# A two-layer trunk kernel: the blocked down-projection over 20 tiles of features in one pass, sums of activations made in the up-projection

## Chip, cores and metric

The kernel runs on one core of a Trainium2 chip. The metric is the device time of one execution in microseconds (us); lower is better.

## What is computed

The reference is a two-layer trunk over 1024 prompt tokens and 8 x 4 sample tokens, 1056 columns in all, with a model width of 1024. In each layer a mixer, a cross-attention and a convolutional feed-forward part follow one another. The change concerns the feed-forward part alone:

```python
def conv_ffn(h, w_up, conv_w, conv_b, w_down, prev):
    L = h.shape[1]
    up = h @ w_up                                  # 1024 -> 2 * 2816
    ext = jnp.concatenate([prev.astype(up.dtype), up], axis=1)
    c = conv_b + conv_w[0] * ext[:, 0:L]
    for j in range(1, CONV_W):                     # CONV_W = 3
        c = c + conv_w[j] * ext[:, j:j + L]
    a, b = jnp.split(c, 2, axis=-1)
    y = (jax.nn.silu(a) * b).astype(h.dtype)
    return y @ w_down, ext[:, L:]                  # 2816 -> 1024, added to x
```

## The kernel before

Every fp32 product is made of three matmuls (`mm3`): each operand is split into a rounded high part and the low rest, high by high, high by low and low by high (L594, L595, L596). ScalarE (ACT) makes a high part by a copy, VectorE (DVE) the low part by a subtraction.

**Blocks.** In most of the feed-forward part a 2 x 2 block scheme with seven products in place of eight is used. `PRODUCTS` names for each product p the part or sum of weights (a11, a12, s1 to s4, a22), the part or sum of activations (b11, b21, b22, t1 to t4) and the accumulator. Blocks of weights pair two tiles of 128 rows or columns; blocks of activations are half of the 1056 columns (528, two pieces c of 264). The order of the products in a block is p = 1, 2, 6, 5, 7, 3, 4, each for c = 0 and 1: 14 steps. `Blocks.steps` makes the sums of weights on GpSimd (POOL; L233, L234, L235, L239) and their parts (ACT L219, DVE L220); the names are `wru`/`wsu` for raw and summed weights and `whiu`, `wh1u`, `whsu`, `w4u` and so on for parts, with a `d` at the end in the down-projection.

**Up-projection.** 22 tiles of features (f = 0 to 21), each with its gate tile. Tiles 1 to 21 are blocks of 14 steps of 12 matmuls of 128x264 into `blu`. `ffn_take` empties a step's bank into `ext`: ACT copies (L964) after p = 1, 6 and 5, DVE adds (L968) after p = 2, 7 and 3 with a scaling on POOL behind (L969), and one DVE multiply (L966) after p = 4. There are three banks for these, so product 3 waits for the copy that empties product 5. `ffn_conv` queues the convolution of a finished tile in `self.slow`: a first tap on ACT (L1005), two more on DVE (L1008), silu on ACT (L1012) and the product on DVE (L1014, and L1018 for the 32 sample columns), which is stored to `fd` in DRAM. `tick` hands this queue out behind the next tile's steps, by a credit of time. So while PE works on tile f, the other engines convolve tile f - 1.

**Down-projection.** Five groups of four tiles of features (`GROUPS`), each group fetched from `fd`, its seven activation operands made (sums on POOL L723 and L724 and on DVE L726 and L727, parts L519 and L520), and multiplied into four pairs of output tiles: 5 x 4 blocks of 14 steps of 6 matmuls, 1680 a layer, into `bld`. `ffn_add` adds every step's bank to the residual rows `xff`, once or twice: on DVE (L984), or for p = 1 and 6 by an ACT copy into `dtd` (L981) and a POOL add (L982). The last two tiles of features (20 and 21) follow in `out_last` (`ogd_e`), which isn't changed.

Programs are written in the order of the calls; each engine runs its instructions in that order, and DMAs are issued from one queue (SP). Nothing is reordered on the chip.

## Time and profile before

| | |
|---|---|
| median of 3 runs | 3243.94 us (3241.47 to 3248.48) |
| profiled execution | 3238.84 us, of which its span is 3237.1 us |
| up-projection's steady part, layer 0 | within 1100 to 1360 us of the span |
| down-projection by blocks, layer 0 and 1 | from 1399.9 and 2958.4 us to 1633.2 and 3188.6 us |

The span is the time from the first to the last instruction in the trace; 1.7 us of the execution lie around it. PE is TensorE's matmul stream and PEld its weight loads; the trace's times are in us from the start of the span. A row of a timeline gives start, duration, engine, line, operation, written tile, read tiles, shapes, and in square brackets how long the engine stood idle ahead of it and who released it.

### The profile page before, as it was taken

To read this page: it belongs to the slowest core of one execution; us is meant where nothing else is said; L and a number is where in the kernel's file an instruction comes from. 1 tells how busy PE (TensorE), PEld (TensorE's weight loads), DVE (VectorE), ACT (ScalarE), POOL (GpSimd) and SP (SyncE) were. 2 spreads that over 40 slices of the span, in tenths; PEclk is the share of its full clock that TensorE was granted. 3 is DMA by queue.
4 is the path that set the end of the run, shared out by engine and by line. 5 is a ranking of instruction groups with operands and counts; after the bars stand their busy time and mean duration, and the time that the engine had idled before them with its cause. 6 is when DMAs were issued, how large, how long until landed. Compare 5 with 4: busy or idle time off the path is not lost. (4 is left out here: it accounts for less than half of the span.)

```text
span 3237.1 us, 65350 instructions
## 1 busy us (share of the span) xinstructions
PE 3101.1 (96%) x25741; PEld 2952.3 (91%) x25741; DVE 2446.9 (76%) x4662; ACT 1454.7 (45%) x3008; POOL 1468.3 (45%) x1722
## 2 busy tenths in 40 slices
PE   8999899999989999999999999899999999999998
PEld 6998888998889999988989999889989899999998
DVE  6649977834798888899974444675378988889998
ACT  7223255444464444444442333244445544444445
POOL 5011113300457777778731111240025677777874
PEclk9999999999999999999999999999999999999999
DMA  8513264344222222242231111225333222224322
GB/s 267 187 47 97 80 206 159 107 147 139 89 89 84 82 81 75 74 154 96 83 119 55 47 55 52 76 75 178 111 126 102 73 82 82 79 77 152 101 73 97
DMA packets 367072, 336.08 MB, mean 104 GB/s; under 512 B 30029, under 2 KB 317948, under 8 KB 366764
## 3 DMA queue, kind: packets, MB, share of 16 engines
q1 hardware_dynamic: 366764, 331.90, 32.1%
q8 instruction: 202, 3.31, 0.4%
q14 instruction: 106, 0.87, 0.1%
HBM read 250.60 MB, written 81.24 MB: 103 GB/s over the span
## 5 line engine op out<-in xcount | busy, mean ns | idle before, releaser
L969 POOL TENSOR_TENSOR ext<-ext,rstdff 128x264 f32<-128x264 f32 (+2 forms) x336 | 358.7, 1093 | 122.2 <-DVE ext L968 121.9
L1008 DVE SCALAR_TENSOR_TENSOR ct<-ext,cw,ct 128x528 f32<-128x528 f32 (+1 forms) x352 | 370.5, 1089 | 47.4 <-ACT ct L1005 45.6
L1005 ACT ACTIVATE ct<-ext,cw 128x544 f32<-128x544 f32 (+1 forms) x176 | 141.7, 833 | 212.1 <-POOL ext L969 96.2
L596 PE MATMUL blu<-hhff,wlou 128*128 128x264 f32 x672 | 191.8, 286 | 3.6 <-DVE wlou L220 3.6
L594 PE MATMUL blu<-hhff,whiu 128*128 128x264 f32 x672 | 191.5, 286 | 0.0
L982 POOL TENSOR_TENSOR xff<-xff,dtd 128x264 f32<-128x264 f32 x160 | 159.8, 1011 | 63.8 <-ACT dtd L981 63.0
L723 POOL TENSOR_TENSOR o<-o 128x528 f32<-128x528 f32 x4 | 5.4, 1342 | 360.1 <-DVE xo1bb L272 179.4
L984 DVE TENSOR_TENSOR xff<-xff,bld 128x264 f32<-128x264 f32 x400 | 154.3, 417 | 6.7 <-PE bld L596 5.2
L596 PEld LDWEIGHTS blu<-hhff,wlou 128*128 128x128 f32 x672 | 127.2, 189 | 4.0 <-DVE wlou L220 4.0
L964 ACT COPY ext<-blu 128x264 f32<-128x264 f32 (+2 forms) x336 | 98.3, 323 | 65.0 <-PE blu L596 62.9
L594 PEld LDWEIGHTS blu<-hhff,whiu 128*128 128x128 f32 x672 | 127.5, 190 | 0.0
L594 PE MATMUL pjxq<-hhxa,whxq 128*128 128x352 f32 x384 | 126.3, 329 | 0.0
L595 PE MATMUL pjxq<-hlxa,whxq 128*128 128x352 f32 x384 | 125.5, 327 | 0.0
L596 PE MATMUL pjxq<-hhxa,wlxq 128*128 128x352 f32 x384 | 124.8, 325 | 0.0
L968 DVE TENSOR_TENSOR ext<-ext,blu 128x264 f32<-128x264 f32 (+2 forms) x336 | 104.4, 350 | 0.0
L595 PE MATMUL blu<-hhff,whiu 128*128 128x264 f32 x336 | 96.6, 288 | 0.0
L596 PE MATMUL blu<-hhff,w4u 128*128 128x264 f32 x336 | 95.7, 285 | 0.0
L595 PE MATMUL blu<-hlff,w4u 128*128 128x264 f32 x336 | 95.7, 285 | 0.0
L594 PE MATMUL blu<-hhff,w4u 128*128 128x264 f32 x336 | 95.6, 285 | 0.1
L595 PE MATMUL blu<-hlff,whiu 128*128 128x264 f32 x336 | 95.6, 285 | 0.0
L219 ACT CAST w4u<-wru 128x512 fp32r<-128x512 f32 x42 | 26.1, 621 | 149.9 <-POOL wru L239 141.6
L1400 POOL TENSOR_TENSOR khg<-khg,tothg 128x512 f32<-128x512 f32 (+1 forms) x24 | 31.8, 1325 | 123.1 <-PE shg L1371 53.1
(2690 smaller groups left out, 13083.5 us busy)
## 6 DMA issues: line engine op xcount, KB each, us to landing
wru<-in_ffn_w_up SPq DMA_DIRECT2D x88, 512.0 KB
wrd<-in_ffn_w_down SPq DMA_DIRECT2D x80, 256.0 KB
wrkv<-in_xa_w_kv SPq DMA_DIRECT2D x32, 512.0 KB
kc<-in_cache_mem_k SPq DMA_DIRECT2D x64, 256.0 KB
vc<-in_cache_mem_v SPq DMA_DIRECT2D x64, 256.0 KB
fd<-ct SPq DMA_DIRECT2D x44, 264.0 KB
fd<-ct SPq DMA_DIRECT2D x44, 248.0 KB
xmx<-xd SPq DMA_DIRECT2D x16, 528.0 KB
```

Of the source, the lines that this page charges most:

```text
L219: nc.scalar.copy(out=hi, in_=src)
L594: nc.tensor.matmul(ps, wh, ah, start=first, stop=False, **kw)
L595: nc.tensor.matmul(ps, wh, al, start=False, stop=False, **kw)
L596: nc.tensor.matmul(ps, wl, ah, start=False, stop=last, **kw)
L964: nc.scalar.copy(out=d, in_=z)
L968: nc.vector.tensor_tensor(out=d, in0=d, in1=z, op=ALU.add)
L969: nc.gpsimd.tensor_tensor(out=d, in0=d, in1=r, op=ALU.mult)
L982: nc.gpsimd.tensor_tensor(out=x, in0=x, in1=b, op=ALU.add)
L984: nc.vector.tensor_tensor(out=x, in0=x, in1=ps, op=ALU.add)
L1005: nc.scalar.activation(out=ct[q], in_=exts[q][0][:, o:o + w], func=AF.Identity, scale=wv(0, q), bias=wv(3, q))
L1008: nc.vector.scalar_tensor_tensor(out=ct[q], in0=exts[q][0][:, o + j:o + j + w], scalar=wv(j, q), in1=ct[q], op0=ALU.mult, op1=ALU.add)
L1400: nc.gpsimd.tensor_tensor(out=kv, in0=kv, in1=tv[:, :, 1:2].to_broadcast([P, nb, m]), op=ALU.mult)
```

## The change

The down-projection by blocks is one pass over the 20 tiles: `DOWN` puts its seven products outermost; for each there are two halves of the output (`mp`, two pairs of output tiles) and three cuts of the ten pairs of features (`CUTS`: 4, 3 and 3). A product accumulates over all ten pairs in its own banks, and only then `take` adds it to the residual: 48 adds on DVE into `xff`, 16 into `ud` and 16 ACT copies into `ud`, and 8 POOL adds of 528 columns in a layer stand for the 200 DVE and 80 POOL adds of 264 columns and the 80 ACT copies of before. There are still 1680 matmuls a layer. The weights come in pieces of 384 or 512 KB, and since a piece serves one product, some blocks are loaded two or three times: 23.6 MB for 10.5 MB a layer. Sums of weights on POOL and the columns of their parts stay as many.

The sums of activations t1 to t4 are made in the up-projection, as 40 instructions of 128x528 a layer on POOL: one for an even tile (`first_sum`), three for an odd one (`other_sums`), put into `self.slow` ahead of the next tile's convolution. The seven operands are stored to DRAM (`bd`) as 7 x 10 half blocks of 270 KB, and fetched and split product by product (5 fetches of 540 KB and 10 splits of 528 columns for each), one product ahead. The 80 such sums of before in the down-projection (half on POOL, half on DVE, both layers) fall away.

```diff
...
-NSLOT = 40
+NSLOT = 43
...
-GROUPS = [2,2,2,2,2]
+
+NPAIR = 10
+DOWN = (1, 2, 5, 6, 3, 7, 4)
+CUTS = ((0, 4), (4, 3), (7, 3))
...
-PREP = {(0, 2): 1, (1, 3): 2, (1, 10): 1, (2, 3): 1, (2, 8): 1, (2, 11): 1, (3, 0): 1, (3, 4): 1, (3, 10): 1, (3, 12): 1}
...
+class Down:
...
+        self.at = [(p, mp, j) for p in DOWN for mp in range(2) for j in range(len(CUTS))]
...
+    def load(self, i):
+        if i >= len(self.at):
+            return
+        k = self.k
+        p, mp, j = self.at[i]
+        n = CUTS[j][1] * 256
+        names = {1: ("a11",), 2: ("a12",), 5: ("a21", "a22"), 6: ("a11",), 3: ("a12",), 7: ("a21", "a11"), 4: ("a22",)}[p]
+        t = k.wp.tile([P, 1024], F32, tag="wraw", name=f"wrd{self.l}_{i}", bufs=3)[:, :n]
+        self.raw[i] = t
+        if len(names) == 2:
+            self.s[mp, j] = k.c(f"sd{self.l}_{i}")[:, :n]
+            self.block(names[0], i, self.s[mp, j])
+        self.block(names[-1], i, t)
...
+    def sums(self, i):
...
+        gt = self.k.nc.gpsimd.tensor_tensor
+        r, s = self.raw[i], self.s.get((mp, j))
+        if p == 5:
+            gt(out=s, in0=s, in1=r, op=ALU.add)
+        elif p == 6:
+            gt(out=s, in0=s, in1=r, op=ALU.subtract)
+        elif p in (3, 7):
+            gt(out=r, in0=r, in1=s, op=ALU.subtract)
...
+    def parts(self, i):
...
+        src = self.s[mp, j] if p in (5, 6) else r
+        n = CUTS[j][1] * 256
+        hi, lo = (k.wp.tile([P, 1024], F32R, tag=q, name=f"{q}d{self.l}_{i}", bufs=2)[:, :n] for q in ("whi", "wlo"))
+        nc.scalar.copy(out=hi, in_=src)
+        nc.vector.tensor_tensor(out=lo, in0=src, in1=hi, op=ALU.subtract)
...
+    def split(self, x, q):
...
+        r = self.yr.pop((x, q))
+        nm = f"y{PRODUCTS[DOWN[x]][1]}{self.l}{q}"
+        hi, lo = (k.c(f"{nm}{a}", F32R)[:, :2 * H] for a in "hl")
+        for s in (slice(0, H), slice(H, 2 * H)):
+            nc.scalar.copy(out=hi[:, s], in_=r[:, s])
+            nc.vector.tensor_tensor(out=lo[:, s], in0=r[:, s], in1=hi[:, s], op=ALU.subtract)
...
+    def take(self, p, m, c, ps):
...
+        x, y, u = k.x[m], k.x[m + 4], self.u[m // 2][:, m % 2 * H:(m % 2 + 1) * H]
+        uc = u[:, c * HC:(c + 1) * HC]
+        if p == 1:
+            nc.scalar.copy(out=uc, in_=ps)
+            add(tt, x[:, cs(0)], ps)
+        elif p == 2:
+            add(tt, x[:, cs(0)], ps)
+        elif p == 5:
+            add(tt, x[:, cs(1)], ps)
+            add(tt, y[:, cs(1)], ps)
+        elif p == 3:
+            add(tt, x[:, cs(1)], ps)
+        elif p == 4:
+            add(tt, y[:, cs(0)], ps)
+        else:
+            add(tt, uc, ps)
+            if c == 1:
+                for t in ((x[:, H:T],) if p == 6 else (y[:, H:T], y[:, 0:H])):
+                    add(gt, t, u)
...
+    def run(self):
...
+            if j == 0:
+                pool, tag = ((k.acc, "a"), (k.mps, "m"))[mp]
+                banks = {(m, c): pool.tile([P, 512], F32, tag=tag, name=f"bd{self.l}{p}{mp}{m}{c}")[:, :HC] for c in range(2) for m in range(2)}
+            wh, wl = self.wt.pop(i)
+            acts = self.acts[x]
+            us = 6 * n * HC / 2400.0
+            for c in range(2):
+                for m in range(2):
+                    for q in range(n):
+                        ah, al = (t[:, c * HC:(c + 1) * HC] for t in acts[k0 + q])
+                        k.mm3(banks[m, c], wh[:, q, m * P:(m + 1) * P], wl[:, q, m * P:(m + 1) * P], ah, al,
+                              k0 + q == 0, k0 + q == NPAIR - 1)
+                    if j == len(CUTS) - 1:
+                        self.take(p, 2 * mp + m, c, banks[m, c])
+                if c == 0:
+                    if i == 0:
+                        self.split(0, 4)
+                        self.fetch(1, 0)
+                    self.parts(i + 1)
+                    self.load(i + 3)
+                else:
+                    self.sums(i + 2)
+                    if e < np_ - 1:
+                        self.split(x + 1, e)
+                    self.fetch(*((x + 1, e + 1) if e < np_ - 1 else (x + 2, 0)))
+                k.tick(us - 0.9)
+                yield i
...
-                    groups[0].run({2: 1, 9: 2, 10: 1, 12: 1}.get(s, 0))
+                    down.ahead(s)
...
-        for u, (g, m, w) in enumerate(dns):
-            t = self.c(f"dt{w.name}") if SLOWADD else None
...
+        for i in down.run():
+            if i == 3 and self.cst:
+                self.conv_state_out(l, NFT - NFT % 4)
+            elif i == 6 and not last:
+                self.tick(1e9)
+                self.conv_last(l)
+                last = [0]
+            elif i == len(down.at) - 4 and last == [0]:
+                last = self.ffn_rest(l, at)
...
+        def store(nm, t):
+            self.dma(self.bd[nm][pair // 2][pair % 2], t)
...
-                nc.vector.tensor_tensor(out=b[:, :n], in0=a[:, :n], in1=b[:, :n], op=ALU.mult)
-                self.dma(self.fd[f][:, o:o + n], b[:, :n])
+                if f >= 2 * NPAIR:
+                    d, e = b, a[:, :TS]
+                elif h == 0:
+                    self.rows[odd] = b, a
+                    d = b
+                else:
+                    d = self.rows[odd][1]
+                    e = d[:, n:H]
+                nc.vector.tensor_tensor(out=d[:, :n], in0=a[:, :n], in1=b[:, :n], op=ALU.mult)
                 if h:
                     js = [t[:, (CW - H) * q + TP + 2 - H:][:, :NS * (LS + 2)].rearrange("p (s j) -> p s j", j=LS + 2)[:, :, :LS] for q in range(2)]
-                    nc.vector.tensor_tensor(out=a[:, :TS].rearrange("p (s j) -> p s j", j=LS), in0=js[0], in1=js[1], op=ALU.mult)
-                    self.dma(self.fd[f][:, TP:], a[:, :TS])
+                    nc.vector.tensor_tensor(out=e.rearrange("p (s j) -> p s j", j=LS), in0=js[0], in1=js[1], op=ALU.mult)
+                if f >= 2 * NPAIR:
+                    self.dma(self.fd[f][:, o:o + n], d[:, :n])
+                    if h:
+                        self.dma(self.fd[f][:, TP:], e)
+                elif odd or not h:
+                    store(("b11", "b12", "b21", "b22")[2 * odd + h], d)
             return [(0.0, first)] + [(0.65, lambda j=j, q=q: more(j, q)) for j in (1, 2) for q in range(2)] + [(0.8, product)]
-        self.slow += half(0) + half(1)
+        def first_sum():
+            a, b = self.rows[0]
+            gt(out=a, in0=b, in1=a, op=ALU.subtract)
+            store("t1", a)
+
+        def other_sums():
+            (a, b), (c, d) = self.rows[0], self.rows[1]
+            gt(out=b, in0=d, in1=b, op=ALU.subtract)
+            store("t3", b)
+            gt(out=d, in0=d, in1=a, op=ALU.subtract)
+            store("t2", d)
+            gt(out=c, in0=c, in1=d, op=ALU.subtract)
+            store("t4", c)
+        gt = nc.gpsimd.tensor_tensor
+        self.slow += self.sums + half(0) + half(1)
+        self.sums = [(0.0, other_sums if odd else first_sum)] if f < 2 * NPAIR else []
...
+    nc = bacc.Bacc("TRN2", target_bir_lowering=False, num_devices=1, dynamic_dma_scratch_size=1024)
```

On POOL, tile 19 of layer 0's up-projection, before: the sums of weights (`wru`, `wsu`), the scalings of `ext` after product 2 (x2), the sum for product 3 (L239), and the scalings after product 7.

```order
L233 TENSOR_TENSOR wsu_19_15574<-wru_190_15322,wru_191_15506 128x512
L234 TENSOR_TENSOR wru_191_15506<-wru_191_15506 128x512
L235 TENSOR_TENSOR wsu_19_15574<-wru_191_15506,wru_190_15322 128x512
L969 TENSOR_TENSOR ext_15512<-ext_15512,rstdff_10921 128x264 x2
L239 TENSOR_TENSOR wru_190_15322<-wru_190_15322,wsu_19_15574 128x512
L933 MEMSET ext_15772 128x2
L934 COPY ext_15772<-cst_14614 128x8x2
L933 MEMSET ext_15775 128x2
L934 COPY ext_15775<-cst_14614 128x8x2
L969 TENSOR_TENSOR ext_15515<-ext_15515,rstdff_10921 128x264
```

The same place after the change, where L1103 is the scaling, L241 the sum for product 3, and L1179, L1181 and L1183 are the sums of activations of an odd tile:

```order
L235 TENSOR_TENSOR wsu_19_15629<-wru_190_15377,wru_191_15559 128x512
L236 TENSOR_TENSOR wru_191_15559<-wru_191_15559 128x512
L237 TENSOR_TENSOR wsu_19_15629<-wru_191_15559,wru_190_15377 128x512
L1103 TENSOR_TENSOR ext_15565<-ext_15565,rstdff_10936 128x264 x2
L1179 TENSOR_TENSOR ct_15331<-ct_15587,ct_15331 128x528
L241 TENSOR_TENSOR wru_190_15377<-wru_190_15377,wsu_19_15629 128x512
L1181 TENSOR_TENSOR ct_15587<-ct_15587,ct_15331 128x528
L1067 MEMSET ext_15826 128x2
L1068 COPY ext_15826<-cst_14658 128x8x2
L1067 MEMSET ext_15829 128x2
L1068 COPY ext_15829<-cst_14658 128x8x2
L1183 TENSOR_TENSOR ct_15587<-ct_15587 128x528
```

One sum now stands between the scalings and the sum for product 3, and two behind that one. In even tiles there is one sum (L1174), at the first of these places. The order is this one in both layers from about the fifth tile on.

On ACT, the same tile before: the cast of `w4u` reads the sum L239, and behind it the copies empty product 5 (c = 1).

```order
L964 COPY ext_15515<-blu_1820_15631 128x264
L219 CAST w4u_19_15750<-wru_190_15322 128x512
L964 COPY ext_15515<-blu_1821_15653 128x232
L964 COPY ext_15515<-blu_1821_15653 128x8x4
L219 CAST whsu_19_15733<-wsu_19_15574 128x1024
L1005 ACTIVATE ct_15792<-ext_15512,cw_10715 128x528
L1005 ACTIVATE ct_15831<-ext_15512,cw_10715 128x544
```

After the change:

```order
L1098 COPY ext_15568<-blu_1820_15685 128x264
L221 CAST w4u_19_15804<-wru_190_15377 128x512
L1144 ACTIVATE ct_15852<-ext_15565,cw_10730 128x528
L1098 COPY ext_15568<-blu_1821_15707 128x232
L1098 COPY ext_15568<-blu_1821_15707 128x8x4
L221 CAST whsu_19_15787<-wsu_19_15629 128x1024
L1151 ACTIVATE ct_15852<-ct_15852 128x528
L1144 ACTIVATE ct_15891<-ext_15565,cw_10730 128x544
```

A first tap of the convolution (L1144, 528 columns) has moved ahead of these copies, between them and the cast.

On DVE in the down-projection, before (layer 0, third group; L984 adds a bank to the residual, L220 makes low parts of weights, L520 those of activations):

```order
L984 TENSOR_TENSOR xff_5_16536<-xff_5_16536,bld_4400_17508 128x264
L984 TENSOR_TENSOR xff_5_16536<-xff_5_16536,bld_4401_17517 128x264
L984 TENSOR_TENSOR xff_6_16537<-xff_6_16537,bld_4611_17693 128x264
L520 TENSOR_TENSOR y08t11l<-y08r_17260,y08t11h 128x528 x2
L220 TENSOR_TENSOR wlod_80_17732<-wrd_800_17538,whid_80_17731 128x512
L984 TENSOR_TENSOR xff_7_16538<-xff_7_16538,bld_4620_17723 128x264
L984 TENSOR_TENSOR xff_7_16538<-xff_7_16538,bld_4621_17735 128x264
L220 TENSOR_TENSOR wl1d_80_17759<-wrd_801_17652,wh1d_80_17758 128x512
L984 TENSOR_TENSOR xff_7_16538<-xff_7_16538,bld_4600_17655 128x264
L984 TENSOR_TENSOR xff_7_16538<-xff_7_16538,bld_4601_17670 128x264
L520 TENSOR_TENSOR y08t00l<-y08r_17254,y08t00h 128x528 x2
L984 TENSOR_TENSOR xff_6_16537<-xff_6_16537,bld_4620_17723 128x264
```

After the change (product 5; L373 adds to the residual, L336 and L358 make the low parts):

```order
L373 TENSOR_TENSOR xff_3_16594<-xff_3_16594,bd_17197 128x264
L358 TENSOR_TENSOR yt200l<-yrt_17364,yt200h 128x528 x2
L373 TENSOR_TENSOR xff_2_16593<-xff_2_16593,bd_17198 128x264
L373 TENSOR_TENSOR xff_3_16594<-xff_3_16594,bd_17199 128x264
L336 TENSOR_TENSOR wlod_13_17395<-sd_13_17287,whid_13_17394 128x768
L358 TENSOR_TENSOR yt201l<-yrt_17433,yt201h 128x528 x2
L336 TENSOR_TENSOR wlod_14_17454<-sd_14_17340,whid_14_17453 128x768
L358 TENSOR_TENSOR yt202l<-yrt_17486,yt202h 128x528 x2
L336 TENSOR_TENSOR wlod_15_17511<-sd_15_17399,whid_15_17510 128x1024
L373 TENSOR_TENSOR xff_0_16591<-xff_0_16591,bd_17366 128x264
L373 TENSOR_TENSOR xff_4_16595<-xff_4_16595,bd_17366 128x264
L373 TENSOR_TENSOR xff_1_16592<-xff_1_16592,bd_17367 128x264
```

The adds now come at the end of a product's half alone, with the low parts between them.

## Rows read from the trace of the kernel before

**Rows 1.** Page part 4: the chain that ended last, shares of the span by engine.
```profile
DVE 2%; PE 2%; issue 1%; POOL 0%; DMA 0%; ACT 0%; DVEq 0%; SPq 0%; POOLq 0%
```

**Rows 2.** Windows: up-projection of layer 0, then the start of its down-projection.
```profile
core 0: us, PE busy (x) PEld busy (x) DVE busy (x) ACT busy (x) POOL busy (x), PEclk, DMA share, GB/s
1100.00:1360.00 260.00, 260.00 (x2126) 259.16 (x2125) 220.57 (x323) 121.06 (x225) 198.69 (x258) 1.00 0.27 81
1400.00:1440.00 40.00, 33.10 (x233) 31.68 (x232) 36.27 (x59) 16.59 (x36) 31.48 (x34) 0.88 0.39 145
```

**Rows 3.** Windows: each layer's first down-projection matmul to the last two tiles' first.
```profile
1399.90:1633.20 233.30, 213.70 (x1650) 207.74 (x1648) 221.59 (x376) 105.04 (x228) 179.15 (x178) 0.97 0.31 103
2958.40:3188.60 230.20, 212.75 (x1647) 206.90 (x1647) 220.19 (x373) 105.36 (x228) 178.89 (x176) 0.98 0.31 101
```

**Rows 4.** Waits in 1400 to 1640, us in total, times, longest.
```profile
PE bld L596 <- DVE wlod L220: 7.8, 7, 2.0
```

**Rows 5.** Lines by form in 1400 to 1640: busy us, mean ns, idle before.
```profile
L984 DVE TENSOR_TENSOR xff<-xff,bld 128x264 f32<-128x264 f32 x198 | 76.4, 417 | 3.7 <-PE bld L596 3.0 <-POOL xff L982 0.6
...
L982 POOL TENSOR_TENSOR xff<-xff,dtd 128x264 f32<-128x264 f32 x80 | 79.6, 1008 | 33.6 <-ACT dtd L981 33.3
...
L724 POOL TENSOR_TENSOR y08r<-y08r,y08r 128x528 f32<-128x528 f32 x2 | 3.6, 1784 | 0.0
L724 POOL TENSOR_TENSOR y04r<-y04r,y04r 128x528 f32<-128x528 f32 x2 | 2.8, 1412 | 0.0
```

**Rows 6.** Window with the greatest traffic in the trace: DMA share and GB/s last.
```profile
2950.00:2970.00 20.00, 15.59 (x112) 14.96 (x110) 18.83 (x28) 10.48 (x22) 13.71 (x17) 0.91 0.89 340
```

**Rows 7.** Timeline of DVE in one up-projection tile: start, duration, operation.
```profile
1306.26 0.70 DVE L1014 TENSOR_TENSOR ct<-ct 128x528 f32<-128x528 f32 x1
1306.88 1.21 DVE L220 TENSOR_TENSOR wl1u<-wru,wh1u 128x1024 fp32r<-128x1024 f32 x1
1308.01 0.66 DVE L1014 TENSOR_TENSOR ct<-ct 128x496 f32<-128x496 f32 x1
1308.60 0.42 DVE L968 TENSOR_TENSOR ext<-ext,blu 128x264 f32<-128x264 f32 x1
1308.94 1.33 DVE L220 TENSOR_TENSOR wlou<-wru,whiu 128x1024 fp32r<-128x1024 f32 x1
1310.19 0.64 DVE L1018 TENSOR_TENSOR ct<-ct 128x32 f32<-128x32 f32 x1
1312.72 0.69 DVE L220 TENSOR_TENSOR w4u<-wru,w4u 128x512 fp32r<-128x512 f32 x1 [1.89 <-ACT w4u L219]
```

**Rows 8.** Timeline of POOL in the same stretch.
```profile
1306.41 4.37 POOL L969 TENSOR_TENSOR ext<-ext,rstdff 128x264 f32<-128x264 f32 x2 [3.06 <-DVE ext L968]
1310.74 1.29 POOL L239 TENSOR_TENSOR wru<-wru,wsu 128x512 f32<-128x512 f32 x1
```

**Rows 9.** Timeline of ACT, then of PE, in the same stretch.
```profile
1312.07 0.62 ACT L219 CAST w4u<-wru 128x512 fp32r<-128x512 f32 x1 [4.10 <-POOL wru L239]
1312.60 0.44 ACT L964 COPY ext<-blu 128x232 f32<-128x232 f32 x2
1315.60 0.83 ACT L1005 ACTIVATE ct<-ext,cw 128x528 f32<-128x528 f32 x1 [1.62 <-DVE wlsu L220]
...
1313.25 0.28 PE L594 MATMUL blu<-hhff,w4u 128*128 128x264 f32 x1
```

**Rows 10.** Waits in 1000 to 1390, up-projection.
```profile
ACT w4u L219 <- POOL wru L239: 71.0, 18, 4.1
...
PE blu L594 <- ACT ext L964: 1.0, 2, 0.7
```

**Rows 11.** Three lines of DVE: duration ns shortest, median, longest.
```profile
L1008 DVE SCALAR_TENSOR_TENSOR ct<-ext,cw,ct x352: 751/985/1833, 972.7 to 3178.0; 128x528 f32<-128x528 f32 x126, 128x544 f32<-128x544 f32 x50
...
L984 DVE TENSOR_TENSOR xff<-xff,bld x400: 407/416/431, 1414.0 to 3196.5; 128x264 f32<-128x264 f32 x134
...
L1018 DVE TENSOR_TENSOR ct<-ct x44: 175/637/1329, 985.1 to 3181.8; 128x32 f32<-128x32 f32 x44
```

More of the change, by code (lines that the diff above doesn't have):

```diff
@@ L250, with __init__ @@
 class Group:
-    def __init__(self, k, name, n, raw=None, src=None):
-        self.k, self.n, self.name, self.src = k, n, name, src
-        self.acts, self.raw = {}, raw or []
-        self.work = ([self.load] if src else []) + [lambda q=q: self.plain(q) for q in range(2 * n)]
+    def __init__(self, k, name, n, raw):
+        self.k, self.n, self.name = k, n, name
+        self.acts, self.raw = {}, raw
+        self.work = [lambda q=q: self.plain(q) for q in range(2 * n)]
         sums = k.act_blocks(self.raw, self.acts, n, self.name)
         self.work += [f for q in sums for f in q]
-    def load(self):
-        k = self.k
-        for q in range(2 * self.n):
-            self.raw.append(k.col(f"{self.name}r{q}"))
-            k.dma(self.raw[q], self.src[q])
     def plain(self, q):
@@ L363, in open @@
         self.kd = [self.drp.tile([256, D], F32, name=f"kd{l}") for l in range(2)]
-        self.fd = [self.drp.tile([P, T], F32, name=f"fd{f}") for f in range(NFT)]
+        self.fd = {f: self.drp.tile([P, T], F32, name=f"fd{f}") for f in range(2 * NPAIR, NFT)}
+        self.bd = {q: [self.drp.tile([2, P, H], F32, name=f"bd{q}{j}") for j in range(NPAIR // 2)] for _, q, _ in PRODUCTS.values()}
         self.vd = [self.drp.tile([256, D], F32, name=f"vd{l}") for l in range(2)]
@@ L799, in ffn @@
         ups = [Blocks(self, f"u{l}_{f}", [w_up[:, (f + ab * NFT) * P:(f + ab * NFT + 1) * P] for ab in range(2)], 4) for f in range(1, NFT)]
-        dns, groups = [], []
-        at = 0
-        for n in GROUPS:
-            g = Group(self, f"y{l}{at}", n, src=self.fd[at:at + 2 * n])
-            groups.append(g)
-            dns += [(g, 2 * m, b) for m, b in enumerate(self.out_sums(w_dn, at, n, f"d{l}_{at}"))]
-            at += 2 * n
-        todo = ups + [q[2] for q in dns]
+        down = Down(self, l, w_dn)
+        at = 2 * NPAIR
+        todo = ups
+        self.sums, self.rows = [], {}
         acts = {"b11": [(rstd.hi[k].h[0], rstd.lo[k].h[0]) for k in range(4)]}
@@ L856, in ffn @@
         last = []
[L857 to L872 removed]
+        for i in down.run():
[7 more added lines that the diff above has]
+                last = self.ffn_rest(l, at)
+            yield
         self.tick(1e9)
@@ L994, in ffn_conv @@
             nc.gpsimd.tensor_copy(out=self.cst[f // 4][1][:, q, :, f % 4].rearrange("p (s j) -> p s j", j=2), in_=es[:, :, LS:LS + 2])
+        pair, odd = f // 2, f % 2
+        def store(nm, t):
+            self.dma(self.bd[nm][pair // 2][pair % 2], t)
         def half(h):
@@ L2244 @@
     from concourse.bass_utils import run_bass_kernel_spmd
-    nc = bacc.Bacc("TRN2", target_bir_lowering=False, num_devices=1)
+    nc = bacc.Bacc("TRN2", target_bir_lowering=False, num_devices=1, dynamic_dma_scratch_size=1024)
     arrays, ins, outs = {}, {}, {}
```

59 lines of the change are left out of this document (45 added, 14 removed).

## The prediction

> **What bounds the kernel now.** I read the chain that ended last first: only DVE and PE have a share of it worth the name [rows 1]. Then the windows of the two stages. The up-projection's steady part holds 2126 matmuls in 260 us with PE busy throughout at a granted clock of 1.00 [rows 2]: 8.18 a microsecond, so PE is the bound there, with nothing to gain. In the two down-projections 1650 and 1647 matmuls, nearly all of the same 128x264 form, take 463.5 us [rows 3]. At 8.18 they would take 403, so **60 us are lost in the down-projections**. DVE is busy for 441.8 of the 463.5 us and PE for 426.5 [rows 3]. The waits name DVE too: the low parts of weights keep PE [rows 4], because they stand in DVE's queue among 198 additions of 0.417 us, 76.4 us in all [rows 5].
>
> **The down-projection after.** A layer has 64 DVE additions from a bank in place of 200: 136 x 0.417 = 57 us less. Its 20 sums on DVE go too. Low parts of weights and activations keep their columns, so DVE falls from 221 us a layer to some 150 or less, in about 202 us of PE. On POOL, 80 additions of 1.01 us [rows 5] become 8 of twice the columns, and 20 sums leave. On ACT, 80 copies become 16. No engine but PE is then near its limit, and what is late next is a matmul.
>
> What takes some of the 60 us back:
> - **The start.** Before, the first 40 us hold 33.1 us of PE at a clock of 0.88 [rows 2]: 6.9 us lost, part of the 60. After, the first activations are fetched and split, and the first weights made, in the last up-projection tile too, now ten halves and two blocks of weights. I take 5 us a layer, 10 in all, between 0 (the queues have room) and 25 (the whole preparation shows).
> - **DMA.** Products 5 and 7 load two blocks of weights, 5.2 MB, and each product fetches the next one's 2.7 MB: 7.9 MB in 240 matmuls, 29.3 us, which is 270 GB/s. The greatest rate in the trace is 340 GB/s [rows 6]: the transfers need 23 us at that rate and are hidden. At 240 GB/s they would take 33 us, 3.7 us beyond their cover, 15 us over the four. I take 0.
> - **Banks.** The two halves of a product write different banks, so the additions at a half's end have the next half, about 15 us, as cover: nothing.
>
> I forecast a gain of 60 - 10 = **50 us** here, between 30 and 60.
>
> **The up-projection after.** This is where the change pays. The 40 sums a layer have 528 columns. Such sums on POOL took 1.41 us on average where POOL was mostly undisturbed and 1.78 beside DVE [rows 5]. The question is what stands behind them. Read the three engines together around 1311 us [rows 7 to 9]. POOL waits 3.06 us for DVE, scales twice in 4.37 us, and makes the sum for product 3, 512 columns in 1.29 us, until 1312.03. (528 columns are then 1.3 us at best.) ACT had stood idle for 4.10 us for it, casts, and then copies product 5's second piece out of its bank, until 1313.04. PE's product 3, second piece, starts at 1313.25: **0.2 us of slack**. ACT waits like this in 18 places for 71.0 us in the up-projection, while PE waits for its copies for 1.0 us in all [rows 10]. This is also a closed loop: the second piece of product 3 goes through DVE's addition, POOL's scaling and the convolution on ACT and DVE, and the addition that POOL waits 3.06 us for in the next tile comes behind the convolution in DVE's queue. So a delay is not made up for in the next tile.
>
> The order of the changed kernel puts one sum of activations on exactly this path, ahead of the sum for product 3, in even and odd tiles alike: +1.3 us. And on ACT the first tap, 0.83 us [rows 9], now stands between the cast and the copies. Together 1.3 + 0.83 - 0.2 = 1.9 us of PE waiting a tile. The other two sums of an odd tile come behind, 2.6 us on POOL ahead of the scalings after product 7, where POOL now has some idle time; I add 0.2 us a tile on average. **2.1 us x 20 tiles x 2 layers = 84 us.** Lower bound 0: two taps of the convolution, 2 x 0.75 [rows 11], also move forward on DVE, into the 1.89 us in which it waits for that cast [rows 7], and what they free could shorten the loop by as much as the sum lengthens it. Upper bound: 2.6 us a tile, two sums on average. I stay near the upper end because DVE and POOL hold each other up in just these microseconds. While DVE runs its L1014 and L220 back to back, two scalings take 4.37 us; the 32-column product L1018 takes 0.64 us beside them, 0.175 at its shortest [rows 7, 8, 11]; a tap takes 0.75 to 1.83 us [rows 11]. DVE's additions from a bank don't stretch at all, 0.407 to 0.431 us [rows 11]. A sum on POOL is so not in idle time only: it delays DVE's work with two operands in SBUF as well.
>
> The Trainium skill ("SBUF — State Buffer", "SBUF: two separate sides") says that VectorE's instructions with two inputs in SBUF and GpSimd's share one port pair as an exclusive lock, held for the whole instruction, while the other fully blocks. The stretched rows above agree with it, L1018 most plainly. By that rule an added sum of 1.3 us is 1.3 us that neither engine can use, and where they already take turns without a gap it would lengthen each tile by the 2.6 us of my upper bound.
>
> The added stores, 18.9 for 10.8 MB a layer over 430 us, add some 19 GB/s to 81 [rows 2]: hidden.
>
> **The sum.** 3238.8 - 50 + 84 = 3273 us. This stands against the profiled execution, 3238.8 us, which is 5 us below the median of the three runs shown; beside that median the same step would be 3278 us.
>
> **Rivals.**
> 1. *The loop takes the sums up.* PE never waits in the up-projection, as the 3.06 us and more of POOL's idle time in each tile would suggest; ACT's tap is early and does no harm. What speaks against it is the 0.2 us of slack. Then 3239 - 50 = 3189 us. This ends on the other side; it decides once less than 50/40 = 1.25 us a tile is lost.
> 2. *Half of it.* The taps that move forward give back about 1 us in each tile: 1.1 x 40 = 44, so 3233 us, a little faster or no change.
> 3. *DVE and POOL have no gap left.* 2.6 us a tile, and 0.3 for the moved tap: 2.9 x 40 = 116; 3305 us. POOL is busy for 76% and DVE for 85% of the steady part [rows 2], much of it stretched by the other, so there is some gap; against it.
> 4. *The down-projection doesn't give its gain.* If products 5 and 7 wait for DMA and the start costs 25 us, 60 - 25 - 15 = 20 us are gained: 3239 - 20 + 84 = 3303 us. Or DVE is still late: its splits now come evenly, against that.
>
> **How the numbers follow.** My forecast, 1.7 to 2.5 us a tile and 40 to 60 us gained, has 0.52 and lies between 3247 and 3299 us. Rival 1 has 0.13, rival 2 0.20, rivals 3 and 4 together 0.15. A change under 0.2%, 6.5 us, can't be told from none. Faster: 0.13 and about half of rival 2, 0.24. Same: 0.07, from rival 2 and the lower edge of the forecast. Slower: 0.69. The range leaves out most of rival 1 and the far half of 3 and 4: 3208 to 3308 us.
>
> **What would show it.** In the up-projection's steady part the period of a tile goes from 20.7 to about 22.7 us and PE is busy for some 91%, waiting for the ACT copy after product 5 ahead of the second piece of product 3. The cast of `w4u` waits for POOL still longer, and the sums take 1.3 to 1.8 us. In the down-projection, from the first matmul into `bd` to the first into `ogd_e`, there are some 207 us a layer with PE near 98% and DVE under 75%. I am wrong if the period stays under 21.5 us, if PE waits for something else there (the cast whsu, or a bank held by DVE), or if the down-projection takes over 215 us.

## The result: 0.9% slower, and the profile after

The changed kernel takes 3273.9 us (median of four executions, 3271.2 to 3276.7) against 3243.8 us (four, 3241.5 to 3248.5): a ratio of 1.0091 with a 95% interval of 1.0073 to 1.0108. The profiled execution took 3276.3 us, its span 3274.6, 37.5 more than before.

First the chain that ended last, from the page of the changed kernel: shares of the span by engine, to be held against [rows 1].

```profile
PE 53%; DVE 23%; POOL 11%; issue 6%; ACT 4%; DMA 3%; SPq 0%; DVEq 0%; POOLq 0%; ACTq 0%
```

Then its windows: the steady part of layer 0's up-projection, the last 40 us of it, and each layer's down-projection by blocks (first matmul into `bd` to first into `ogd_e`) in three stretches. Columns as in [rows 2].

```profile
1100.00:1360.00 260.00, 242.79 (x1937) 237.27 (x1937) 200.85 (x294) 111.80 (x206) 207.86 (x256) 1.00 0.28 89
1400.00:1440.00 40.00, 38.63 (x312) 38.04 (x311) 33.80 (x52) 21.70 (x42) 25.52 (x32) 1.00 0.49 168
1442.40:1500.00 57.60, 57.20 (x468) 56.98 (x467) 36.33 (x59) 27.25 (x45) 6.10 (x6) 1.00 0.81 270
1500.00:1535.00 35.00, 31.11 (x231) 30.53 (x230) 28.11 (x30) 11.86 (x18) 24.46 (x11) 0.90 0.83 269
1535.00:1656.30 121.30, 120.49 (x989) 120.28 (x988) 81.00 (x97) 39.37 (x57) 47.22 (x24) 1.00 0.50 162
3014.50:3072.00 57.50, 56.54 (x464) 56.33 (x463) 36.59 (x58) 27.16 (x45) 5.67 (x6) 1.00 0.78 259
3072.00:3107.00 35.00, 30.58 (x234) 29.95 (x233) 26.83 (x31) 11.83 (x18) 23.13 (x10) 0.95 0.83 271
3107.00:3230.80 123.80, 121.55 (x991) 120.71 (x990) 79.99 (x97) 39.63 (x57) 46.84 (x25) 1.00 0.48 156
```

A tile of the up-projection has 168 matmuls, so a window's count gives the **period**: 168 x 260 / 2126 = 20.55 us before [rows 2], 168 x 260 / 1937 = 22.55 after. Forty tiles at 2.00 us are 80 us. The blocks of the up-projection, first to last, took 445.2 and 445.6 us in the two layers and now take 486.1 and 485.3: **80.6 us lost**. The down-projections by blocks take 213.9 and 216.3 us in place of 233.3 and 230.2 [rows 3]: 33.3 gained. From there on, to the next layer's tiles and to the end, another 11.4 are gained, in part because some 30 of the 1680 block matmuls of a layer ran behind the first one of the last two tiles before ([rows 3] has 1650 and 1647) and none does now. **44.7 us gained** in all; the program's start differs by 1.5.

Now one odd tile of the changed kernel, the place of [rows 7 to 9]: timelines of POOL, DVE, ACT and PE. L1179 and L1181 are sums of activations, L241 is the sum for product 3, L221 the cast of `w4u`, L1144 the first tap, L1098 the copies after product 5, L738 the first matmul of product 3's second piece. Two rows of L241 stand ahead, of the tiles before.

```profile
1277.92 1.28 POOL L241 TENSOR_TENSOR wru<-wru,wsu 128x512 f32<-128x512 f32 x1
...
1301.17 1.29 POOL L241 TENSOR_TENSOR wru<-wru,wsu 128x512 f32<-128x512 f32 x1
...
1317.61 3.24 POOL L1103 TENSOR_TENSOR ext<-ext,rstdff 128x264 f32<-128x264 f32 x2 [3.06 <-DVE ext L1102]
1321.03 2.18 POOL L1179 TENSOR_TENSOR ct<-ct,ct 128x528 f32<-128x528 f32 x1 [0.19 <-DVE ct L1164]
1323.17 1.28 POOL L241 TENSOR_TENSOR wru<-wru,wsu 128x512 f32<-128x512 f32 x1
1324.41 1.30 POOL L1181 TENSOR_TENSOR ct<-ct,ct 128x528 f32<-128x528 f32 x1
...
1326.97 1.32 POOL L1183 TENSOR_TENSOR ct<-ct 128x528 f32<-128x528 f32 x1
1328.26 2.87 POOL L1103 TENSOR_TENSOR ext<-ext,rstdff 128x264 f32<-128x264 f32 x3
...
1320.81 1.21 DVE L222 TENSOR_TENSOR wlou<-wru,whiu 128x1024 fp32r<-128x1024 f32 x1
...
1324.49 0.62 ACT L221 CAST w4u<-wru 128x512 fp32r<-128x512 f32 x1 [4.97 <-POOL wru L241]
1325.01 0.82 ACT L1144 ACTIVATE ct<-ext,cw 128x528 f32<-128x528 f32 x1
1325.74 0.42 ACT L1098 COPY ext<-blu 128x232 f32<-128x232 f32 x2
...
1326.21 0.39 PE L738 MATMUL blu<-hhff,w4u 128*128 128x264 f32 x1 [1.16 <-ACT ext L1098]
```

Read it backwards from the last row. PE stood idle for 1.16 us for a copy; the copy stood behind the tap, the tap behind the cast, the cast had waited 4.97 us for L241, and L241 came directly behind the sum L1179. That sum ran beside DVE's `wlou` and took 2.18 us; the next, L1181, ran while DVE waited and took 1.30.

The waits of the changed kernel in 1100 to 1360 us (us in total, times, longest) name the same copies, and for PE's matmuls only one wait more, of 0.4 us for an addition. Of the 17 waits of PE, 11 are at this place, 1.1 us in odd tiles and 1.6 in even ones; the other six are of 0.2 us, ahead of product 6:

```profile
ACT w4u L221 <- POOL wru L241: 56.6, 11, 5.3
...
PEld blu L738 <- ACT ext L1098: 20.4, 17, 1.8
...
PE blu L738 <- ACT ext L1098: 16.7, 17, 1.6
```

In the down-projection, product 5: ACT, DVE, POOL, then PE. L357 and L358 split activations of the next product, L335 casts weights, L336 makes the low part from such a cast, L740 needs it, and L322 on POOL makes sums of weights.

```profile
1514.83 1.17 ACT L357 CAST yt202h<-yrt 128x528 fp32r<-128x528 f32 x2 [4.96 <-DMA yrt<-bdt]
1515.90 1.04 ACT L335 CAST whid<-sd 128x1024 fp32r<-128x1024 f32 x1
...
1515.50 3.29 DVE L358 TENSOR_TENSOR yt202l<-yrt,yt202h 128x528 fp32r<-128x528 f32 x2 [3.01 <-ACT yt202h L357]
1518.71 2.83 DVE L336 TENSOR_TENSOR wlod<-sd,whid 128x1024 fp32r<-128x1024 f32 x1
...
1518.19 5.05 POOL L322 TENSOR_TENSOR sd<-sd,wrd 128x768 f32<-128x768 f32 x2
...
1517.48 0.28 PE L739 MATMUL bd<-yt100l,whid 128*128 128x264 f32 x1
1521.60 0.59 PE L740 MATMUL bd<-yt100h,wlod 128*128 128x264 f32 x1 [3.84 <-DVE wlod L336]
1521.99 0.42 PE L738 MATMUL bd<-yt100h,whid 128*128 128x264 f32 x1
```

ACT waited 4.96 us for a transfer that nobody needed yet, with the cast that PE needed queued behind. The cast ended at 1516.94, but its low part only at 1521.54: DVE's two instructions took 6.0 us together, while POOL made sums of weights beside them. Elsewhere in this trace two such splits take 1.33 us and a subtraction of 1024 columns 1.21. At those lengths the low part would have been there at about 1518.2, and PE would have idled for some 0.5 us (an estimate from these rows). So the late transfer and the hold-up of DVE beside POOL both have a part in PE's 3.84 us without work. PE's matmuls then ran at 0.42 us apiece in place of 0.28 for a while: the granted clock is 0.50, the lower level of 1.2 GHz, in 1521.6 to 1526, and its mean 0.90 in 1500 to 1535; in the stretches on either side it is 1.00.

### The profile page after: what moved, and what is told of

The parts are those of the page before. It is cut to its first block, busy times and chain, and to the rows that moved or that the text cites. A ratio compares the mean times of both kernels' runs of the same rounds, so it can differ in the third digit from the quotient of the medians.

```text
span 3274.6 us, 64326 instructions
## 1 busy us (share of the span) xinstructions
PE 3106.0 (95%) x25741; PEld 2953.0 (90%) x25741; DVE 2283.7 (70%) x4274; ACT 1400.5 (43%) x2788; POOL 1347.3 (41%) x1514
## 4 chain that ended last, share of the span: by engine, by line
PE 53%; DVE 23%; POOL 11%; issue 6%; ACT 4%; DMA 3%; SPq 0%; DVEq 0%; POOLq 0%; ACTq 0%
DVE ct L1147 5%; POOL ext L1103 5%; PE bd L740 3%; PE bd L738 3%; PE bd L739 3%; ACT ct L1144 2%; PE pjxq L738 2%; PE pjxq L739 2%; PE pjxq L740 2%; PE blu L738 1%; DVE ct L1161 1%; PE blu L740 1%; PE blu L739 1%; POOL wru L241 1%; DVE ext L1102 1%
## 5 line engine op out<-in xcount | busy, mean ns | idle before, releaser
L1103 POOL TENSOR_TENSOR ext<-ext,rstdff 128x264 f32<-128x264 f32 (+2 forms) x336 | 311.3, 950 | 166.3 <-DVE ext L1102 166.1
L1144 ACT ACTIVATE ct<-ext,cw 128x544 f32<-128x544 f32 (+1 forms) x176 | 140.9, 831 | 191.4 <-POOL ext L1103 128.0
L738 PE MATMUL blu<-hhff,whiu 128*128 128x264 f32 x672 | 191.8, 286 | 0.0
L740 PE MATMUL blu<-hhff,wlou 128*128 128x264 f32 x672 | 190.9, 285 | 0.0
L738 PE MATMUL blu<-hhff,w4u 128*128 128x264 f32 x336 | 99.3, 296 | 46.6 <-ACT ext L1098 46.6
L336 DVE TENSOR_TENSOR wlod<-wrd,whid 128x768 fp32r<-128x768 f32 (+1 forms) x60 | 79.5, 1326 | 72.7 <-ACT whid L335 72.2
L738 PEld LDWEIGHTS blu<-hhff,whiu 128*128 128x128 f32 x672 | 127.5, 190 | 0.0
L740 PEld LDWEIGHTS blu<-hhff,wlou 128*128 128x128 f32 x672 | 127.0, 189 | 0.0
L738 PE MATMUL pjxq<-hhxa,whxq 128*128 128x352 f32 x384 | 126.3, 329 | 0.0
L740 PE MATMUL pjxq<-hhxa,wlxq 128*128 128x352 f32 x384 | 125.0, 325 | 0.0
L1098 ACT COPY ext<-blu 128x264 f32<-128x264 f32 (+2 forms) x336 | 96.6, 321 | 60.8 <-PE blu L740 60.6
L335 ACT CAST whid<-wrd 128x768 fp32r<-128x768 f32 (+1 forms) x60 | 54.2, 907 | 139.1 <-PE bd L739 112.9
L738 PEld LDWEIGHTS blu<-hhff,w4u 128*128 128x128 f32 x336 | 63.2, 188 | 54.3 <-ACT ext L1098 54.3
L222 DVE TENSOR_TENSOR w4u<-wru,w4u 128x512 fp32r<-128x512 f32 x42 | 37.2, 886 | 103.8 <-ACT w4u L221 103.8
L221 ACT CAST w4u<-wru 128x512 fp32r<-128x512 f32 x42 | 26.0, 619 | 184.4 <-POOL wru L241 184.4
L740 PE MATMUL blu<-hhff,w4u 128*128 128x264 f32 x336 | 95.4, 284 | 0.0
```

What stands on the lines that cost most here:

```text
L222: nc.vector.tensor_tensor(out=lo, in0=src, in1=hi, op=ALU.subtract)
L335: nc.scalar.copy(out=hi, in_=src)
L336: nc.vector.tensor_tensor(out=lo, in0=src, in1=hi, op=ALU.subtract)
L738: nc.tensor.matmul(ps, wh, ah, start=first, stop=False, **kw)
L740: nc.tensor.matmul(ps, wl, ah, start=False, stop=last, **kw)
L1098: nc.scalar.copy(out=d, in_=z)
```

## The experiments

Two theories of the 2 us a tile were tried against each other. **A, the place:** a sum costs what it delays L241 by, since the cast, the tap, the copies and PE follow one another without slack; anything as long at that place costs the same. **B, the port:** a sum costs because POOL and DVE, each with two operands in SBUF, hold each other up, wherever it stands. Windows below are all of 1100 to 1360 us, with the columns of [rows 2]; "before" is the kernel before, run beside the experiment. Where a single time is given, the kernel ran once, with its profile.

**1. Without the sums** (`e1_no_sums`): the four `gt(...)` lines of `first_sum` and `other_sums` go, the stores stay.

> The changed kernel without its 80 sums of activations on POOL (what is stored as t1 to t4 is not summed, so the output is not the reference's); the stores and all else stay, the first tap on ACT still stands between the cast of w4u and the copies. Theory A (place): the sum ahead of the sum for product 3 and the moved tap delay the copies; without the sum 0.83 - 0.2 = 0.6 us a tile are left, so about 3274 - 80 + 25 = 3219 us. Theory B (port): DVE and POOL have no time left on their shared way to SBUF; with the sums gone all of the up-projection's loss goes, about 3194 us. A third view, that the sums cost nothing and the tap or the stores do: 3260 us or more.

3214.2 us against 3246.7. Its window, then three rows of its POOL timeline:

```profile
1100.00:1360.00 260.00, 256.49 (x2079) 253.78 (x2079) 209.58 (x317) 120.49 (x224) 174.79 (x243) 1.00 0.31 97
```

```profile
1276.82 1.28 POOL L241 TENSOR_TENSOR wru<-wru,wsu 128x512 f32<-128x512 f32 x1 [1.33 <-DVE wlou L222]
...
1297.87 1.30 POOL L241 TENSOR_TENSOR wru<-wru,wsu 128x512 f32<-128x512 f32 x1 [1.33 <-DVE wlou L222]
...
1318.98 1.28 POOL L241 TENSOR_TENSOR wru<-wru,wsu 128x512 f32<-128x512 f32 x1 [1.33 <-DVE wlou L222]
```

The period is 21.01 us. The sums so cost 22.55 - 21.01 = 1.54 us a tile, and 0.46 of the 2.00 remain without them. The starts of L241 divide the 1.54. From the odd tile's to the next even tile's there are 21.05 us here and 23.25 with the sums; from the even to the odd one, 21.11 and 22.00. The one sum ahead of L241 thus costs 0.9 us in the odd tile; if it costs as much in the even one, the two more of an odd tile (2.2 - 0.9) cost 1.3 together, or 0.65 a tile. The rows also show a wait that the trace of before doesn't have: without a sum, L241 waits 1.33 us for DVE's `wlou`, which reads what L241 overwrites. Before, the scalings took 4.37 us and ended at 1310.78, behind `wlou` at 1310.27 [rows 7, 8]; now they take 3.24 and end first.

**2. Fills in place of the sums** (`e2_fill`): POOL writes constants, with no operand to read; not the sums.

```diff
-            gt(out=a, in0=b, in1=a, op=ALU.subtract)
+            fill(a)
...
+        def fill(t):
+            for w in (528, 528, 64):
+                nc.gpsimd.memset(t[:, :w], 0.0)
```

> Each sum is replaced by three fills of 528, 528 and 64 columns on POOL, which write and read nothing (the output is not the reference's). A fill of 512 columns took 0.53 us in the trace of before, so POOL is held about 1.1 us ahead of the sum for product 3. Theory A (place): the delay counts, whatever POOL does in it; 1.1 + 0.83 - 0.2 = 1.7 us a tile, 3194 + 68 = 3262 us. Theory B (port): what costs is that sums and DVE's two-operand work take turns; fills that don't hold DVE up cost little, 3194 to 3220 us.

3215.7 us against 3246.7, x2066, a period of 21.14: as good as none, and within what B expected. POOL's timeline from an even tile over an odd one to the next even one, then `wlou` of the odd tile on DVE:

```profile
1299.54 1.28 POOL L241 TENSOR_TENSOR wru<-wru,wsu 128x512 f32<-128x512 f32 x1 [0.18 <-DVE wlou L222]
...
1316.54 3.23 POOL L1103 TENSOR_TENSOR ext<-ext,rstdff 128x264 f32<-128x264 f32 x2 [3.05 <-DVE ext L1102]
1319.72 1.98 POOL L1187 MEMSET ct<- 128x528 f32 x4
1321.66 1.28 POOL L241 TENSOR_TENSOR wru<-wru,wsu 128x512 f32<-128x512 f32 x1
...
1341.05 1.14 POOL L1187 MEMSET ct<- 128x528 f32 x2
...
1319.75 1.21 DVE L222 TENSOR_TENSOR wlou<-wru,whiu 128x1024 fp32r<-128x1024 f32 x1
```

The fills run beside `wlou` at their own length, in the time in which L241 has to wait for it. In an even tile two of them, 1.14 us, don't delay L241 at all: it still waits 0.18 us for `wlou`. In an odd tile there are 1.9 us from the scalings' end to L241, against 1.3 without sums. The expectation of A was worked out without that wait, so its miss of 46 us is not all evidence against A. But the sums had the same wait to lie in. Ahead of L241 a sum starts 0.19 us behind the scalings; at its 1.30 us alone it would end 0.16 us past that wait (an estimate from these rows). Beside `wlou` it takes 2.18, ends 1.19 us behind `wlou`, and L241 starts 2.3 us behind the scalings, 1.0 later than without sums. So at this place the length of a sum alone would cost next to nothing, and some 0.85 of the 1.0 us is that the sum is held up beside `wlou`. This is B, at the place that A names.

**3. Sums on DVE** (`e3_sums_dve`): `gt = nc.vector.tensor_tensor` for these four.

> The same sums, on DVE instead of POOL, at the place where they were emitted, ahead of the low part of w4u, where DVE waits for 1.9 us in each tile. Theory A (place): POOL's path is free; the tap's 0.6 us a tile remain: 3219 us, or 3194 if the tap costs nothing. Theory B (port): a DVE sum holds the port about half as long as one on POOL, so about half of the 80 us stay: 3235 us.

3238.4 us against 3246.7, x2008, 21.75 us: nearer B's 3235 than A's 3219. Better than on POOL by 0.8 us a tile, though DVE was the busier of the two before [rows 2]. One of the sums waits for a transfer here (see 8).

**4. The cast of `w4u` late** (`e4_w4_late`): the cast is queued behind that of `whsu`, its low part behind the additions after product 3, so that the copies after product 5 don't wait for L241.

```diff
+        with k.tc.issue_after(late[0].ins) if late else nullcontext():
+            k.cast = nc.scalar.copy(out=hi, in_=src)
+        with k.tc.issue_after(late[1].ins) if late else nullcontext():
             nc.vector.tensor_tensor(out=lo, in0=src, in1=hi, op=ALU.subtract)
...
```

> The sums stay on POOL. The cast of w4u (it belongs to the next tile) is queued on ACT behind the copies out of product 5's bank and the cast of whsu, and its low part on DVE behind the additions of product 3; the build then also puts all sums behind the sum for product 3 and the tap behind the copies. Theory A (place): nothing on the path any more, 3194 us. Theory B (port): the sums still need 2 x 1.3 us a tile of a port with about 1.5 to 2 us free: 40 us of the 80 stay, 3235 us.

3253.2 us against 3246.7, x1984, 22.02 us, slower than either theory had it. Only 0.5 us a tile is won back. PE's waits, of the same stretch:

```profile
PE blu L745 <- ACT ext L1105: 8.3, 13, 1.2
...
PE blu L745 <- DVE ext L1109: 3.8, 6, 0.7
```

And POOL in an odd tile:

```profile
1313.48 1.72 POOL L244 TENSOR_TENSOR wru<-wru,wsu 128x512 f32<-128x512 f32 x1
1315.33 1.34 POOL L1187 TENSOR_TENSOR ct<-ct,ct 128x528 f32<-128x528 f32 x1
1317.90 1.32 POOL L1189 TENSOR_TENSOR ct<-ct,ct 128x528 f32<-128x528 f32 x1 [1.23 <-DMA bdb<-ct]
1319.30 1.67 POOL L1191 TENSOR_TENSOR ct<-ct 128x528 f32<-128x528 f32 x1
1320.93 1.11 POOL L1111 TENSOR_TENSOR ext<-ext,rstdff 128x264 f32<-128x264 f32 x1
```

All three sums now stand behind the sum for product 3 (L244), with a wait for a store among them, and the next scaling comes behind them. PE waits less, but now for copies and for additions. Taking one link off the path is not enough while POOL makes the sums.

**5 and 6. The place alone, in the kernel before.** Work that needs nothing and that nothing reads is put on POOL between the scalings and L239 of every up-projection tile: two fills of 528 columns (`e5_before_fill`), or an addition of 416 columns with two operands in SBUF (`e6_before_tt`).

```diff
+                    with k.tc.issue_after(k.scaled.ins):
+                        for _ in range(2):
+                            i = k.nc.gpsimd.memset(k.scratch, 0.0)
+                    with k.tc.issue_after(i.ins):
+                        gt(out=a[:, w:], in0=a[:, w:], in1=self.s[:, :w], op=ALU.subtract)
...
```

In the other, the loop is one `gt` on `scratch[:, :416]`.

> The kernel before, with two fills of 528 columns on POOL (about 1.07 us, no operand read) put between the scalings after product 2 and the sum for product 3 in each of 40 tiles; nothing else moves on any engine. Theory A (place): this is a pure delay on the path with 0.2 us of slack: 0.87 us a tile, +35 us, 3278 us. Theory B (port): a fill holds up no DVE instruction, and the loop has more slack than the one tile showed: under +10 us.

> The same place and about the same length, but an addition of 416 columns that reads two operands from SBUF (0.175 + 416 x 0.00215 = 1.07 us, from the 256- and 512-column sums of the trace). Theory A (place): the same +35 us as the fills. Theory B (port): clearly more than the fills; the 0.9 us that it holds the port is added to each tile, +36 us, with the fills near 0. Both at once: fills +20 to 35, addition +45 to 60.

3278.6 and 3275.6 us against 3242.2 (twelve executions, 3238.6 to 3248.4): 36 and 33 us slower. The fills take 1.13 us together (POOL timeline):

```profile
1323.30 4.37 POOL L978 TENSOR_TENSOR ext<-ext,rstdff 128x264 f32<-128x264 f32 x2 [3.06 <-DVE ext L977]
1327.61 1.13 POOL L242 MEMSET scratch<- 128x528 f32 x2
1328.71 1.30 POOL L244 TENSOR_TENSOR wru<-wru,wsu 128x512 f32<-128x512 f32 x1
```

Less the 0.2 us of slack, 0.93 x 40 = 37 us, and 36 came. The addition takes 0.88 us at its median, 0.68 x 40 = 27, and 33 came. This is A with nothing else changed: work at this place costs its own length. The slack of 0.2 us, read off one tile, was right, and the loop of rival 1 gives nothing back. B is not tested here: in the kernel before, `wlou` has ended 0.5 us before the scalings do [rows 7, 8], so the addition has no such subtraction beside it and is not stretched (0.88 us at its median, 0.87 at its shortest). In the changed kernel the sums do.

**7. Neither sums nor the early cast** (`e7_no_sums_late`): the edits of 1 and 4 together, so the sums are left out.

> Without the sums (output not the reference's), and with the cast of w4u and its low part queued late, so that the moved tap stands behind the copies. If the 20 us that the kernel without sums kept above 3194 us come from the tap's place on ACT, this is 3192 to 3198 us; if they come from DVE's new order or from the stores, 3210 us or more.

3187.3 us against 3242.2, and PE is never idle:

```profile
1100.00:1360.00 260.00, 260.00 (x2135) 259.79 (x2135) 237.18 (x324) 126.17 (x228) 193.29 (x259) 1.00 0.31 100
```

A period of 20.46. The 0.46 us a tile that stayed without the sums belong to the cast with the tap behind it, ahead of the copies. With the up-projection at about the rate of before (20.46 us a tile for 20.55, some 4 us of it), the new down-projection leaves the kernel 55 us faster.

**8. Sums on DVE and the late cast** (`e8_dve_late`): 3 and 4 together.

> Both changes that helped: the sums on DVE, where they hold the port half as long, and the cast and low part of w4u late, so that DVE doesn't wait 1.9 us for a cast and can make the sums in that time. If port time and waits are what is left: 3194 to 3205 us, faster than both kernels. If the gains don't add: 3225 us or more.

3253.1 us (nine executions, 3250.2 to 3258.6) against 3242.2: a ratio of 1.0031 (1.0020 to 1.0041), where some 50 us less were expected. The DVE timeline of an odd tile:

```profile
1317.79 0.71 DVE L1189 TENSOR_TENSOR ct<-ct,ct 128x528 f32<-128x528 f32 x1 [1.72 <-DMA bdb<-ct]
...
1319.16 0.83 DVE L1109 TENSOR_TENSOR ext<-ext,blu 128x264 f32<-128x264 f32 x3
```

The sum t2 is written over b22, whose store has to land first. DVE waits 1.72 us for that, with the additions L1109 behind it, which empty the banks that PE waits for. A wait for a transfer costs the whole queue behind it, here as on ACT in product 5.

**9, 10 and 11. Two sums a tile.** t2 is written over t1, which is stored a tile earlier, and t4 is made one tile later. With the late cast and the sums on DVE (`e9_dve_late_22`), the same with the sums on POOL (`e10_pool_late_22`), and on DVE with the cast where the change has it (`e11_dve_22`).

```diff
-            gt(out=d, in0=d, in1=a, op=ALU.subtract)
-            store("t2", d)
-            gt(out=c, in0=c, in1=d, op=ALU.subtract)
-            store("t4", c)
+            gt(out=a, in0=d, in1=a, op=ALU.subtract)
+            store("t2", a)
+            self.left.append((a, c, store))
...
```

> As the previous one with the sums on DVE and late w4u, but t2 is written over t1 instead of over the b22 half that is just being stored, so no sum waits for that store, and t4 is made one tile later, so every tile has two sums. If the 3253 us of the previous version came from that wait (1.7 us in odd tiles, with the urgent additions queued behind it) and from three sums in a row: even tiles there took 20.6 us, so odd ones should too or take about a microsecond more: 3192 to 3215 us, faster than both kernels. If port time in sum is what is short: 3230 us or more.

> The same, with the sums on POOL, behind the sum for product 3. A POOL sum holds the port about 1.13 us, a DVE sum about 0.57. If port time is short: two a tile cost about 1 us a tile more than on DVE, 3230 to 3250 us. If only waits and places counted: the same as on DVE.

> Sums on DVE, two a tile and without the wait for the store, but the cast and low part of w4u where the changed kernel has them. If the place on ACT counts on top: between the 3238 us of the plain move to DVE and the late version, some 3225 us; if late w4u hurts rather than helps, it is the fastest of the three.

On DVE 3226.0 us (five executions, 3224.2 to 3228.5) against 3246.2 (nine), a ratio of 0.9935 (0.9921 to 0.9949); on POOL 3258.5; on DVE without the late cast 3231.1, so the late cast does no harm there. The windows, of DVE and POOL with the late cast:

```profile
1100.00:1360.00 260.00, 254.19 (x2054) 250.74 (x2054) 247.88 (x333) 121.35 (x223) 184.05 (x243) 1.00 0.29 95
```

```profile
1100.00:1360.00 260.00, 247.43 (x1980) 242.18 (x1979) 225.51 (x298) 116.20 (x214) 205.86 (x258) 1.00 0.28 92
```

21.27 and 22.06 us. The edits of these two differ in the sums' engine alone, and in both the copies don't wait for L241, so A by itself would have them alike. This speaks for B too: off that path, two sums a tile on POOL cost 0.8 us more than on DVE. No wait for a store is left that could be the reason; that POOL's next scalings stand behind the sums, 1.3 us each there, could be, and no run parts the two.

**12. The sums held back** (`e12_dve_hold`): as 9, and a tile's two sums are queued on DVE behind the additions out of product 4's banks.

```diff
+                if s == 13:
+                    while self.held:
+                        with self.tc.issue_after(self.p4.ins):
+                            self.held.pop(0)()
...
```

> As the fastest version so far (3226 us), but the two sums of a tile are queued on DVE behind the additions out of product 4's banks, instead of ahead of the additions after product 7, for which PE still waited there. If the queue ahead of those additions is what the rest of the loss comes from (0.7 us a tile): 3198 to 3212 us. If DVE, busy 95% of the time there, is the bound whatever the order: 3220 to 3232 us.

**3211.7 us** (four executions, 3209.6 to 3216.0) against 3246.5 (seven): a ratio of 0.9896 (0.9878 to 0.9913), faster than both kernels. Its window, and the only wait of PE's matmuls that the view lists there:

```profile
1100.00:1360.00 260.00, 255.91 (x2082) 253.71 (x2082) 248.43 (x337) 123.89 (x227) 197.56 (x243) 1.00 0.29 95
```

```profile
PE blu L749 <- DVE ext L1117: 4.1, 6, 0.7
```

The period is 20.98 us, 0.43 over that of before. DVE is busy for 96% of the time; whether its load is what remains was not tried.

## Why the prediction was right, step by step

The forecast of 3273 us and its mechanism held: the loss is in the up-projection, at the matmul that was named, through the chain of instructions that was named. That the two parts came so close, 80.6 for 84 and 44.7 for 50, is in part luck, since in each of them some terms were too high and others too low. The terms were these.

- **The up-projection, +84: measured +80.6.** The period went from 20.55 to 22.55 us (from 20.7 to 22.7 in the forecast, though [rows 2] give 20.55), PE to 93% (91). The sums cost 1.54 us a tile, where 1.3 and 0.2 were added; the tap and the cast 0.46, where 0.83 - 0.2 was. Within the 1.54 the two parts were off against each other. The sum ahead of L241 costs 0.9 to 1.0, not 1.3: it takes 2.18 us, but covers the 1.33 for which L241 has to wait for `wlou` anyway, a wait that is new and that the forecast doesn't have. The other two cost about 0.65, not 0.2: the step that "POOL now has some idle time" behind them failed, since L1183 ends at 1328.29 and the next scalings start at once, where the kernel without sums has POOL idle.
- **The port, from which the upper end was argued.** It is there, and on the path: 2.18 us for a sum beside DVE's subtraction `wlou` of 1024 columns against 1.30 alone, and by 2 this hold-up makes some 0.85 of the 1.0 us. So the term of 1.3 was near, but for another reason than its own: the forecast took the sum's own length for the price, with `wlou` over by then as in the kernel before. The Trainium skill ("SBUF — State Buffer", "SBUF: two separate sides") has the port as an exclusive lock between the two engines, and these rows agree. Rival 3, in which the two engines only take turns and a tile loses 2.9 us, did not come about. Where the sums are off the path, the 0.8 us a tile between 9 and 10 is the most that the port can be charged with. The forecast range of 1.3 to 1.8 us for a sum was too narrow.
- **The down-projection, -50: measured -44.7.** At 8.18 matmuls a microsecond the six stretches above miss 0.4, 6.8 and 0.4 us in layer 0, and 0.8, 6.4 and 2.7 in layer 1: 17.4 in all, where 10 were forecast. The division was wrong. The start, taken as 10, costs about 1: the stretches from the first matmul on run at nearly full rate, and in layer 0 the 40 us before them have 312 matmuls, more than the 298 of the steady part's rate. The **DMA term, taken as 0, stands where 13 were lost**, in 1500 to 1535 and 3072 to 3107, where product 5 runs: the transfers run at 270 GB/s, which is the rate that was worked out as needed, but they arrive too late for ACT's splits, and those stand ahead of weight casts in ACT's queue. The sum of bytes was right, and the queue behind a late one was left out; so was DVE, whose two instructions behind it took 6.0 us beside POOL's sums of weights, and the lower clock after the idle time. How the 13 divide among these, no run shows. This is a part of rival 4, at about its price of 15, but in product 5 alone, with more causes than DMA, and without the start's 25 us: product 7 ran without a loss in layer 0. 215 us were set as the bound for being wrong here; the layers came out on either side of it.
- **Banks and stores, 0.** The waits list none of PE for a bank of `bd`, and the traffic of the up-projection went from 81 to 89 GB/s without a wait of PE for a transfer.
- **Rivals 1 and 2**, that the loop gives something back, are excluded by the result, and 5 and 6 show that it gives nothing back for added work.

One sentence ahead of the prediction is wrong: each engine runs its list in order, but the list isn't the order of the calls; the build makes it. The rows of the order are the real lists, so nothing that was read from them changes. But it explains why an experiment that moved one instruction moved others as well: in 4 the edit touches only the cast of `w4u` and its low part, and the sums on POOL moved too. Two counts there, which the prediction repeats, are off as well: the trace has 8 ACT copies into `ud` and 12 POOL additions to `xff` a layer, not 16 and 8. No term of the sum depends on them.

What stays open is why 4 loses 1.56 us a tile against 7 (22.02 and 20.46): the port, or the place that the scheduler then gives the sums. The wait for a store isn't it, since 10 is without one and has 22.06.

## What to carry to other kernels

Work that is moved out of a stage with a crowded engine goes somewhere: look in the receiving stage for what stands directly behind it on its engine, and follow the queue to the bound engine. Here idle time of POOL was no room, because the idle time was itself a wait inside the loop. A wait can hide added work only if that work can run beside what is waited for: fills could, sums that read SBUF beside DVE's subtraction could not. The same work on the busier engine, behind the last urgent instruction of a tile, cost 0.5 us a tile (20.98 against 20.46) in place of 1.5. And a transfer has to be early not only for its reader but for everything queued behind its reader.
